# Sliding windows, 64 x 8 x 8 each, from one core: channel halves on the two partition halves, and stores of one half at a time

## Chip, cores, metric

One NeuronCore of one Trainium2 chip. The metric is the device time of one launch in microseconds; unless said otherwise, the median of several runs. Lower is better.

## The reference

```python
# x: (16, 64, 64, 64) float32;  window_size 8, stride 4  ->  n_h = n_w = 15
for i in range(15):
    for j in range(15):
        result[:, i, j] = x[:, :, 4*i : 4*i + 8, 4*j : 4*j + 8]
# result: (16, 15, 15, 64, 8, 8) float32
```

No arithmetic: 16.8 MB are read once, 59.0 MB written, since windows overlap.

## The kernel before

A partition holds one image b, one half of the channels (ch) and one quarter of the height (q): partition = 8b + 4ch + q. Loads and stores take every fourth partition, so 32 at a time, both halves together.

```python
L = lpool.tile([P, CL, RB, W], f32)          # 128 x (32 channels, 16 rows, 64)
x_v = x.rearrange("b (ch cl) (hq r) w -> hq (b ch) cl (r w)", ch=CH, hq=HQ)
for k in range(NCH):                          # 4 groups of 8 channels
    for q in range(HQ):
        nc.scalar.dma_start(out=L[q::HQ, k*cw:(k+1)*cw, :, :],
                            in_=x_v[q, :, k*cw:(k+1)*cw, :])
for j in range(NW):
    for s in range(NSLOT):                    # window row i = 4q + s
        g = gpool.tile([P, CL, WS, WS], f32, name="g")     # 9 buffers
        # ... VectorE: copy the window; for s = 3 half of it comes from
        #     the next partition by stream_shuffle ...
        for q in range(HQ):
            i = NSLOT * q + s
            if i < NH:
                nc.sync.dma_start(out=o_v[i, j, ...], in_=g[q::HQ, cs, :, :])  # 32 x 8 KB
```

## Time and profile before

| | before |
|---|---|
| time | 222.6 us (221.84 to 222.94) |
| last load packet ends | 45.8 us |
| 8 KB stores | 50.6 to 220.7 us |
| load packet, 4 KB, mean | 164 ns |
| store packet, 8 KB: median, mean | 309, 365 ns |
| store transfers | 237 |

The last five rows come from the trace's packet records (start, duration, size; no engine number). A packet's duration is the time that one of the 16 DMA engines (the page's count) spent on it; in this trace 15.3 packets are under way at a time, on average, from 60 to 200 us. The lines of the page are in the prediction.

### The profile page before, as it was taken

How to read it: one execution, taken by the hardware profiler on the slowest of the kernel's cores; microseconds unless marked ns; L12 is line 12 of the kernel's file. 1: busy time of each engine (PE TensorE's matmuls, PEld its weight loads, DVE VectorE, ACT ScalarE, POOL GpSimd, SP SyncE). 2: the span in 40 equal slices, each digit the busy share in tenths (PEclk: the TensorE clock that was granted, in tenths of full speed). 3: DMA queues.
4: the chain of work that ended last, by engine and by line, in shares of the span. 5: the costliest groups of instructions: out<-in, count | busy, mean ns of one | idle time of the engine just before them, and what ended most of it. 6: DMA issues, size and time to landing. Idle time of an engine off the chain costs nothing.

```text
span 222.1 us, 564 instructions
## 1 busy us (share of the span) xinstructions
DVE 82.9 (37%) x93; POOL 0.2 (0%) x4
## 2 busy tenths in 40 slices
DVE  0000000069946354454526453535454545430000
POOL 0000000000000000000000000000000000000000
DMA  5999999928999999999999999999999999999995
GB/s 210 418 409 412 412 413 409 412 103 285 337 356 351 328 350 344 334 344 337 341 339 348 359 341 342 353 347 335 360 353 342 332 354 334 329 347 335 326 359 215
DMA packets 15733, 75.81 MB, mean 341 GB/s; under 512 B 4049, under 2 KB 4049, under 8 KB 8657
## 3 DMA queue, kind: packets, MB, share of 16 engines
q1 hardware_dynamic: 11376, 59.00, 74.9%
q10 hardware_dynamic: 4352, 16.78, 18.9%
q14 instruction: 5, 0.03, 0.0%
HBM read 16.78 MB, written 58.98 MB: 341 GB/s over the span
## 4 chain that ended last, share of the span: by engine, by line
SPq 59%; DMA 22%; issue 5%; DVE 2%; ACTq 1%; DVEq 0%
SPq L72 59%; DMA L<-in_x_dram 20%; DMA out_dram<-g 3%; ACTq L48 1%; DVE g L64 1%; DVE g L68 1%; DVE g L67 0%; DVEq L64 0%; DVEq L67 0%
## 5 line engine op out<-in xcount | busy, mean ns | idle before, releaser
L64 DVE COPY g<-L 128x2048 f32<-128x2048 f32 (+1 forms) x48 | 55.1, 1159 | 93.2 <-DMA out_dram<-g 47.9
L68 DVE STREAM_SHUFFLE g<-L 128x1024 f32<-128x1024 f32 x15 | 19.2, 1278 | 0.0
L67 DVE COPY g<-L 128x1024 f32<-128x1024 f32 x15 | 10.4, 693 | 21.9 <-DMA out_dram<-g 21.9
L68 DVE LOAD_MASK_SELECT g<-L x15 | 0.2, 15 | 0.0
L92 POOL MEMSET const-bfloat16-1.0<- 128x1 bf16 x1 | 0.1, 102 | 0.0
L92 POOL MEMSET const-uint8-127<- 128x1 uint8 x1 | 0.1, 102 | 0.0
L92 POOL MEMSET const-float32-0.0<- 128x1 f32 x1 | 0.1, 99 | 0.2 <-issue 0.2
L92 POOL MEMSET const-float32-1.0<- 128x1 f32 x1 | 0.1, 99 | 0.0
## 6 DMA issues: line engine op xcount, KB each, us to landing
out_dram<-g SPq DMA_DIRECT2D x221, 256.0 KB, 3.8
L<-in_x_dram ACTq DMA_DIRECT2D x16, 1024.0 KB, 10.8
out_dram<-g SPq DMA_DIRECT2D x16, 64.0 KB, 5.1
```

Of the source, the lines that this page charges most:

```text
L48: nc.scalar.dma_start(out=L[q::HQ, k * cw : (k + 1) * cw, :, :], in_=x_v[q, :, k * cw : (k + 1) * cw, :],)
L64: nc.vector.tensor_copy(out=g[:, cs, :, :], in_=L[:, cs, s * ST : s * ST + WS, cols])
L67: nc.vector.tensor_copy(out=g[:, cs, 0:ST, :], in_=L[:, cs, s * ST : RB, cols])
L68: nc.vector.stream_shuffle(out=g[:, cs, ST:WS, :], in_=L[:, cs, 0:ST, cols], mask=nxt)
L72: nc.sync.dma_start(out=o_v[i, j, :, :, k * CFREE // chunks : (k + 1) * CFREE // chunks], in_=g[q::HQ, cs, :, :],)
L92: nc = _bacc.Bacc("TRN2", target_bir_lowering=False, num_devices=1)
```

## The change

Intent: give the channel half to the upper partition bit and store one half at a time, so that a transfer stays on one partition half (0 to 63 or 64 to 127); let eight of the DMA engines run one group of ten packets behind the other eight, so that the two sets of engines always use different halves; and have fewer, larger stores. That engines on different halves don't hinder each other was the assumption; the trace before has no transfer of one partition half.

```diff
-    x_v = x.rearrange("b (ch cl) (hq r) w -> hq (b ch) cl (r w)", ch=CH, hq=HQ)
+    x_v = x.rearrange("b (ch cl) (hq r) w -> ch hq b cl (r w)", ch=CH, hq=HQ)
+    def load(ch, q, k, b0=0, nb=B):
+        p0 = ch * HP + b0 * HQ + q                  # HP = 64
+        nc.scalar.dma_start(out=L[p0 : p0 + (nb-1)*HQ + 1 : HQ, cs, :, :],
+                            in_=x_v[ch, q, b0 : b0 + nb, cs, :])
+    load(0, *pieces[0], 0, HB)                      # 8 images: eight engines
+    load(0, *pieces[0], HB, HB)
+    for n in range(0, len(pieces), 2):              # then 2 of half 1, 2 of half 0, ...
+        for u in pieces[n : n + 2]:     load(1, *u)
+        for u in pieces[n + 1 : n + 3]: load(0, *u)
...
+    # store: one half of a window, 64 partitions; store_x: crossing windows, 16 partitions
+    J = NW - 1
+    g0, gx = window(J, 0), crossing([J])
+    for b0 in (0, HB):                              # 8 images: eight engines alone
+        store(g0, 0, J, 0, b0, HB)
+        store_x(gx, 0, [J], 0, b0, HB)
+    for j in range(0, J, 2):
+        js = [j, j + 1]
+        gx = crossing(js)
+        for s in range(NSLOT - 1):
+            gs = [window(u, s) for u in js]
+            for ch in (1, 0):                       # 4 + 4 + 2 = 10 packets an engine
+                for u, g in zip(js, gs): store(g, ch, u, s)
+                store_x(gx, ch, js, s)
...  # the last column likewise; window buffers 9 -> 5, two crossing buffers added
```

More of the change, by code (lines that the diff above doesn't have):

```diff
@@ L34 @@
     NSLOT = RB // ST
-    assert WS == 2 * ST
+    CFREE = CL * WS * WS
+    HB = B // 2
+    HP = P // CH
+    assert HQ == 4 and CH == 2 and WS == 2 * ST and HP == B * HQ
     lpool = ctx.enter_context(tc.tile_pool(name="lpool", bufs=1))
-    gpool = ctx.enter_context(tc.tile_pool(name="gpool", bufs=9))
+    gpool = ctx.enter_context(tc.tile_pool(name="gpool", bufs=5))
+    xpool = ctx.enter_context(tc.tile_pool(name="xpool", bufs=2))
     L = lpool.tile([P, CL, RB, W], f32)
-    x_v = x.rearrange("b (ch cl) (hq r) w -> hq (b ch) cl (r w)", ch=CH, hq=HQ)
@@ L43 @@
-    o_v = out.rearrange("b i j (ch cl) r w -> i j b ch (cl r w)", ch=CH)
+    x_v = x.rearrange("b (ch cl) (hq r) w -> ch hq b cl (r w)", ch=CH, hq=HQ)
     NCH = 4
     cw = CL // NCH
-    for k in range(NCH):
-        for q in range(HQ):
-            nc.scalar.dma_start(
-                out=L[q::HQ, k * cw : (k + 1) * cw, :, :],
-                in_=x_v[q, :, k * cw : (k + 1) * cw, :],
-            )
+    def load(ch, q, k, b0=0, nb=B):
+        cs = slice(k * cw, (k + 1) * cw)
+        p0 = ch * HP + b0 * HQ + q
+        nc.scalar.dma_start(
+            out=L[p0 : p0 + (nb - 1) * HQ + 1 : HQ, cs, :, :],
+            in_=x_v[ch, q, b0 : b0 + nb, cs, :],
+        )
@@ L53, with window @@
+    pieces = [(q, k) for k in range(NCH) for q in range(HQ)]
+    load(0, *pieces[0], 0, HB)
+    load(0, *pieces[0], HB, HB)
+    for n in range(0, len(pieces), 2):
+        for u in pieces[n : n + 2]:
+            load(1, *u)
+        for u in pieces[n + 1 : n + 3]:
+            load(0, *u)
+    o_v = out.rearrange("b i j (ch cl) r w -> ch i j b (cl r w)", ch=CH)
     nxt = [min(p + 1, 31) for p in range(32)]
-    CFREE = CL * WS * WS
-    for j in range(NW):
+    def window(j, s):
+        g = gpool.tile([P, CL, WS, WS], f32, name="g")
@@ L56 @@
         cols = slice(j * ST, j * ST + WS)
-        for s in range(NSLOT):
-            g = gpool.tile([P, CL, WS, WS], f32, name="g")
-            chunks = NCH if j == 0 and s == 0 else 1
-            n = CL // chunks
-            for k in range(chunks):
-                cs = slice(k * n, (k + 1) * n)
-                if s < NSLOT - 1:
-                    nc.vector.tensor_copy(out=g[:, cs, :, :], in_=L[:, cs, s * ST : s * ST + WS, cols])
-                else:
-                    nc.vector.tensor_copy(out=g[:, cs, 0:ST, :], in_=L[:, cs, s * ST : RB, cols])
-                    nc.vector.stream_shuffle(out=g[:, cs, ST:WS, :], in_=L[:, cs, 0:ST, cols], mask=nxt)
-                for q in range(HQ):
-                    i = NSLOT * q + s
-                    if i < NH:
-                        nc.sync.dma_start(
-                            out=o_v[i, j, :, :, k * CFREE // chunks : (k + 1) * CFREE // chunks],
-                            in_=g[q::HQ, cs, :, :],
-                        )
+        nc.vector.tensor_copy(out=g[:, :, :, :], in_=L[:, :, s * ST : s * ST + WS, cols])
@@ new lines, in window, with crossing, store @@
+        return g
+    def crossing(js):
+        g = xpool.tile([P, 2, CL, WS, WS], f32, name="gx")
+        for n, j in enumerate(js):
+            cols = slice(j * ST, j * ST + WS)
+            nc.vector.tensor_copy(out=g[:, n, :, 0:ST, :], in_=L[:, :, (NSLOT - 1) * ST : RB, cols])
+            nc.vector.stream_shuffle(out=g[:, n, :, ST:WS, :], in_=L[:, :, 0:ST, cols], mask=nxt)
+        return g
+    def store(g, ch, j, s, b0=0, nb=B):
+        p0 = ch * HP + b0 * HQ
+        o = o_v[ch, s::NSLOT, j].rearrange("q b f -> b q f")[b0 : b0 + nb]
+        nc.sync.dma_start(out=o, in_=g[p0 : p0 + nb * HQ].rearrange("p c r w -> p (c r w)"))
@@ new lines, in store_x @@
+    def store_x(g, ch, js, q, b0=0, nb=B):
+        p0 = ch * HP + b0 * HQ + q
+        o = o_v[ch, q * NSLOT + NSLOT - 1, js[0] : js[-1] + 1].rearrange("j b f -> b j f")[b0 : b0 + nb]
+        i = g[p0 : p0 + (nb - 1) * HQ + 1 : HQ, 0 : len(js)].rearrange("p j c r w -> p j (c r w)")
+        nc.sync.dma_start(out=o, in_=i)
+    J = NW - 1
[9 more added lines that the diff above has]
+            for ch in (1, 0):
+                for u, g in zip(js, gs):
+                    store(g, ch, u, s)
+                store_x(gx, ch, js, s)
@@ L79 @@
+    gx = crossing([J])
+    gs = [window(J, s) for s in range(NSLOT - 1)]
+    for ch, ss in ((1, (0, 1)), (0, (1, 2)), (1, (2,))):
+        for s in ss:
+            store(gs[s], ch, J, s)
+            store_x(gx, ch, [J], s)
 _INS = ['x', 'window_size', 'stride']
```

## The prediction

> **What bounds the kernel now.** The kernel only moves data: 16.8 MB in, 59.0 MB out, one VectorE copy between. I read first the page's parts on busy time and on the 40 slices.
>
> ```profile
> DVE 82.9 (37%) x93; POOL 0.2 (0%) x4
> ...
> DMA  5999999928999999999999999999999999999995
> GB/s 210 418 409 412 412 413 409 412 103 285 337 356 351 328 350 344 334 344 337 341 339 348 359 341 342 353 347 335 360 353 342 332 354 334 329 347 335 326 359 215
> ```
>
> VectorE is idle for 63% of the span, so it doesn't bound. The 16 DMA engines are busy in every slice but one, at two rates: about 412 GB/s while loading (slices 2 to 8), about 342 while storing (slice 11 on). Between them stands one bad slice of 103 GB/s: the last load has landed and no 8 KB store has started. Next I asked for the same by stretch of time (columns: VectorE, GpSimd, clock, DMA share, GB/s).
>
> ```profile
> 3.00:45.00 42.00, 1.28 (x3) 0.00 (x0) 1.00 1.03 412
> 45.00:51.00 6.00, 4.58 (x7) 0.00 (x0) 1.00 0.32 87
> 51.00:220.00 169.00, 77.08 (x84) 0.00 (x0) 1.00 0.96 342
> ```
>
> So 169 of the 222 us are the store stretch: engines 96% busy, yet a sixth slower than in the load. Then the chain that ended last and the waits of SyncE's queue, which issues the stores:
>
> ```profile
> SPq 59%; DMA 22%; issue 5%; DVE 2%; ACTq 1%; DVEq 0%
> ...
> SPq L72 <- DVE g L64: 33.4, 4, 13.7
> SPq L72 <- DMA out_dram<-g: 5.2, 2, 2.6
> ...
> out_dram<-g SPq DMA_DIRECT2D x221, 256.0 KB, 3.8
> L<-in_x_dram ACTq DMA_DIRECT2D x16, 1024.0 KB, 10.8
> ```
>
> SyncE issues without a stop: its waits (33.4 and 5.2 us) all lie before 51 us; from there it issues a 256 KB store every 0.76 us or so, of which the issue itself takes 0.536 at least and 0.644 at the median. 3.8 us from issue to landing over 0.76 is five stores in flight. Two limits are therefore close together: the issue (about 0.64 + 0.045 us between two = 0.68 a store) and the engines.
>
> The trace's packet records tell more. Of 7072 store packets of 8 KB, more than half take exactly 309 ns (26.5 GB/s an engine, 424 on sixteen); the mean is 365, the 90th percentile 514, the longest 944. Load packets of 4 KB: median 159 ns, mean 164, next to none above 172. So a store packet has a clean time of 309 ns and something lengthens about four in ten of them, up to double and more. It is not VectorE: after 200 us, with VectorE done, the mean is still 372 and then 357. Excess: 7072 / 16 = 442 packets an engine x (365 - 309) ns = **24.8 us**. That is what the change can win.
>
> [...] 237 stores left 3792 records of 4 bytes, 16 each.
> [...]
>
> [...] Against it: loads have the same geometry and hardly a slow packet.
>
> **The change part by part.**
> 1. *Partitions.* Channel half goes to the upper partition bit: 64 x half + 4 x image + quarter. [...]
> 2. *Groups.* Two windows (4 + 4 packets an engine) and one crossing store (2) make ten packets of a half, then ten of the other. [...]
> 3. *Stores.* 4 + 7 x 3 x 2 x 3 + 10 = 140 instead of 237. At 0.68 us that is 95 us of issuing, well below the engines' time: SyncE drops out as the second limit, and the queue becomes deeper. Packets: 7200 of 8 KB; engines 0 to 7 take 10 + 420 + 25 = 455, the others 445.
> 4. *Loads.* 33 of 512 KB or less. Engines 0 to 7 take 16 + 31 x 8 = 264 packets of 4 KB x 0.160 = 42.2 us, the others 39.7. From 2.2 us (first packet before) to 44.5; the landing came about 0.4 us after the last packet before: 44.9.
> 5. *Start of the stores.* The stores of the first window's channel chunks during the load are gone; nothing can be stored before all has landed. VectorE then makes the first window (1.23 us), one crossing (0.69 + 1.27 = 1.96), two more crossings (3.9), one window (1.23): the first full group can be issued at 44.9 + 8.3 = 53.2, and its packets start some 1.2 us after the issue (before: 49.4 to 50.6). So 54.4, against 50.6 before: 3.8 us later, only half recovered by work already done (before, 512 packets of 2 KB = 2.7 us an engine were stored by then; after, ten packets = 3.1 us on engines 0 to 7).
> 6. *Steady store.* 445 packets x 309 ns = 137.5; 136 semaphore writes x 15 ns (9 and the gap) = 2.0; first packet unhidden 0.3: 139.8. Buffers do not bind: a pair of columns takes 60 packets = 18.5 us on the engines and 2 x 1.96 + 6 x 1.23 = 11.3 on VectorE; with five window buffers each fill is about 5 us early.
> 7. *End.* 54.4 + 139.8 = 194.2, and 1.4 us from last packet to end of span (220.7 to 222.1 before) = 195.6; the timed median lies 0.5 above the profiled span: **196** if no packet collides.
>
> **Rivals.**
> - *The offset isn't there when it is needed.* By step 5 engines 0 to 7 finish their ten packets near 52, before the first full group: all engines begin it together. If sharing is fair, the offset stays zero and each packet takes 618 ns: 54.4 + 445 x 0.618 = 329 us. But in the kernel before, all 16 engines also start together (50.61 to 50.88), and the mean is 391 ns in the first 10 us and about 360 after[...]. If they do so here by ten packets, the loser stands for about 3 us once: 199.
> - *The slow packets come from writing HBM[...].* Then 365 ns stays: 54.4 + 445 x 0.365 + 3.7 = 220.5, the same time as before. In favour: loads of the same geometry run clean. Pieces in HBM also become 8 KB with jumps, where two neighbours of 16 KB followed one another.
> - *The issue starves the engines.* In favour: SyncE never waits in the store stretch and five stores are in flight, not more. Then slow packets are half-fed ones and the 140 larger stores cure them [...]: 196 to 199 again.
> - *A mix*: collisions of a tenth of the excess to a third remain: 445 x 6 to 19 ns = 3 to 8 us above 196.
>
> **The range.** Two of four stories give 196 to 199, the mix 199 to 204, HBM 220, lasting lockstep 329. That the order of groups was built so exactly for one offset speaks for the clean case, but step 5 says that the offset must form by itself. I take 199, with 192 to 218 for eight in ten; faster by over 2% (below 218.1) 0.79, same 0.08, slower 0.13.
>
> **What would show it.** Right: median store packet 309 and mean below 330; over 400 GB/s in store slices; fewer than 150 store issues and SyncE waiting on landings of stores (queue full) instead of issuing without pause; a hole of some 9 us with little traffic after about 45 us. Wrong: packet mean near 365 (HBM), near 618 at some 215 GB/s (lockstep), load slices well below 400 [...], or VectorE waits of long duration inside a pair of columns with the engines idle (buffers).

An assumption: engines that are at the same partitions at the same time hinder each other, and one a packet ahead is not hindered; what stands after "Against it" speaks against that. In the first rival "sharing" is that two such engines are held up alike, and "do so" that engines get out of step by themselves, both assumptions too; 618 is twice the clean 309.

The sum: 44.5 (end of the loads) + 9.9 (to 54.4, the first full group) + 139.8 (stores) + 1.4 (end) = 195.6, or 196, and 199 with the 3 us of the first rival. How its terms were got: packets an engine are worked out by count, so a store of 64 packets on 16 engines gives four each, and (7200 - 80) / 16 = 445. The sentence cut from step 2 gave the first four stores, of eight images each, to eight engines alone, ten packets each: the offset of one group. The trace before could not show that; the changed kernel's does: 8 records of 4 bytes for each of them in place of 16, and their 80 packets under way eight at a time. The records name no engine: "engines 0 to 7", here and in the expectations, is the name for these eight, taken to be the same each time. "Semaphore writes" are the records of 4 bytes, 9 ns each on average in the trace before; the 6 ns of gap are an estimate: from the end of one 8 KB packet to the start of the next the commonest time there is 2 to 3 ns, and a record of 4 bytes has a gap on either side.

## The result

The changed kernel takes **321.98 us** (320.97 to 327.72, 4 runs, of which the longest counts as slow and is left out of the ratio), the kernel before 222.22 us in the same rounds: 1.449 times as long, with a 95% interval of 1.437 to 1.461. (A ratio is the mean time of one kernel's fast runs over that of the other's of the same rounds, so not quite the ratio of the medians quoted.) The output is correct.

The page of the changed kernel, parts on busy time, slices, the chain that ended last, and issues (issues: count, KB each, us from issue to landing):

```profile
DVE 84.6 (26%) x94; POOL 0.2 (0%) x4
...
DMA  5999999971699999999999999999999999999997
GB/s 156 247 247 245 249 252 250 252 189 78 154 252 239 259 233 262 235 260 233 261 230 266 235 262 237 254 240 260 245 250 252 245 253 242 261 237 258 237 252 182
...
DMA 57%; SPq 17%; DVE 11%; issue 5%; ACTq 2%; DVEq 0%
...
out_dram<-g SPq DMA_DIRECT2D x89, 512.0 KB, 6.5
L<-in_x_dram ACTq DMA_DIRECT2D x31, 512.0 KB, 17.0
```

The engines are as busy as before and move only about 250 GB/s, in the loads too (412 before). The chain has turned from SyncE's issues (59% before) to the transfers (57%). By stretch of time (VectorE, GpSimd, clock, DMA share, GB/s):

```profile
2.00:45.00 43.00, 0.00 (x0) 0.00 (x0) 1.00 0.99 242
45.00:55.00 10.00, 0.00 (x0) 0.00 (x0) 1.00 1.02 244
55.00:320.00 265.00, 84.58 (x94) 0.00 (x0) 1.00 0.94 238
```

At 45 to 55 us, where the kernel before had begun to store, it is still loading at the same low rate. The packet records say what a busy engine was busy with:

| | before | after |
|---|---|---|
| load packet, 4 KB, mean | 164 ns | 264 ns |
| store packet, 8 KB, mean | 365 ns | 516 ns |
| store packets within 312 ns | 60% | 21% |
| store packets of 590 to 630 ns | 2% | 45% |
| last load packet ends | 45.8 us | 73.5 us |
| all 16 engines store from | 50.6 us | 83.1 us |
| last packet | 220.7 us | 319.3 us |

The clean packet is still 309 ns, but the commonest duration is now 596 ns, nearly its double. The 98.6 us between the two last packets divide into 27.7 in the loads (73.5 - 45.8), 4.8 in the gap before the stores (9.6 instead of 4.8) and 66.1 in the stores (236.2 instead of 170.1).

The timeline around the start of the stores (start us, duration us, what):

```profile
74.09 1.23 DVE L75 COPY g<-L 128x2048 f32<-128x2048 f32 x1 [74.09 <-DMA L<-in_x_dram]
...
75.35 0.84 SPq L90 DMA_DIRECT2D out_dram<-g  x1
...
77.15 0.68 SPq L96 DMA_DIRECT2D out_dram<-gx  x1
...
77.88 0.65 SPq L90 DMA_DIRECT2D out_dram<-g  x1
78.58 0.65 SPq L96 DMA_DIRECT2D out_dram<-gx  x1
...
80.56 5.75 DVE L75 COPY g<-L 128x2048 f32<-128x2048 f32 x5
81.80 1.73 SPq L90 DMA_DIRECT2D out_dram<-g  x2
```

The four stores for eight engines alone are issued by 79.2 us, and the packet records show eight packets under way at once, every one within 314 ns, until 80.8 us. The first store for all engines is issued at 81.80 us; its packets begin at 83.07 us on eight engines, 83.3 to 83.6 on the other eight, and from there most of them take about 596 ns (the median from 83.7 to 90 us). So eight engines on one partition half had clean packets, 8 x 8192 bytes / 309 ns = 212 GB/s, and 16 on one half packets of nearly double the time, 16 x 8192 / 596 = 220 GB/s: by this estimate from the packet times, about the same rate for the half. The offset had been worked off before it was needed. In the loads it was not: when all 16 engines became busy at 4.5 us, 81 load packets had begun. Even if all of them were of the eight engines that had begun first, ten each, these had six of their sixteen packets left. e3 and e5 below show what that was worth.

Once the stores run, SyncE is held in the act of issuing (a store of 64 partitions took 0.59 us to issue at least, 1.62 at the median and 2.26 at most):

```profile
101.24 3.46 SPq L90 DMA_DIRECT2D out_dram<-g  x2
104.75 1.76 SPq L96 DMA_DIRECT2D out_dram<-gx  x1
106.56 3.67 SPq L90 DMA_DIRECT2D out_dram<-g  x2
110.27 1.47 SPq L96 DMA_DIRECT2D out_dram<-gx  x1
```

Comparing issue ends with landings, a further store is taken only when two or three are still under way, 6 to 10 packets an engine.

### The profile page after: what moved, and what is told of

It reads as the page before. It is cut to its first block, busy times and chain, and to the rows that moved or that the text cites. A ratio compares the mean times of both kernels' runs of the same rounds, so it can differ in the third digit from the quotient of the medians.

```text
span 320.6 us, 411 instructions
## 1 busy us (share of the span) xinstructions
DVE 84.6 (26%) x94; POOL 0.2 (0%) x4
## 4 chain that ended last, share of the span: by engine, by line
DMA 57%; SPq 17%; DVE 11%; issue 5%; ACTq 2%; DVEq 0%
DMA out_dram<-g 35%; DMA L<-in_x_dram 21%; SPq L96 11%; DVE g L75 8%; SPq L90 7%; DVE gx L84 2%; ACTq L54 2%; DMA out_dram<-gx 1%; DVE gx L83 0%; DVEq L75 0%; DVEq L83 0%
## 5 line engine op out<-in xcount | busy, mean ns | idle before, releaser
L75 DVE COPY g<-L 128x2048 f32<-128x2048 f32 x46 | 56.1, 1227 | 212.0 <-DMA out_dram<-g 126.4
L84 DVE STREAM_SHUFFLE gx<-L 128x1024 f32<-128x1024 f32 x16 | 20.4, 1278 | 0.0
L83 DVE COPY gx<-L 128x1024 f32<-128x1024 f32 x16 | 10.9, 682 | 0.0
```

Source lines behind the costliest of these rows:

```text
L75: nc.vector.tensor_copy(out=g[:, :, :, :], in_=L[:, :, s * ST : s * ST + WS, cols])
L83: nc.vector.tensor_copy(out=g[:, n, :, 0:ST, :], in_=L[:, :, (NSLOT - 1) * ST : RB, cols])
L84: nc.vector.stream_shuffle(out=g[:, n, :, ST:WS, :], in_=L[:, :, 0:ST, cols], mask=nxt)
```

## The experiments

**Words.** A clean packet is one at the commonest short time (159 ns for 4 KB, 309 ns for 8 KB). A run of packets is what an engine takes from one half before it changes to the other. The offset is the number of packets by which the eight engines that take the transfers of eight images are behind the other eight. The records name no engine: packets an engine, runs and offsets are worked out by count, as estimates.

**Theory (partitions).** How long a packet takes depends on the partitions that the other engines are at in the same moment: eight engines on one partition half had packets of 309 ns in the changed kernel, 16 on it 596. Without an offset, by count, all 16 are on one half with nearly every packet. **Rivals:** the HBM addresses of one half are slow; the transfers themselves cost (their size, or those on eight engines); the starts or buffers disturb. In the expectations, a forecast that is not called a rival's, and has lost its reason, is this theory's.

Packet means of all runs, from the trace's packet records:

| run | load ns | store ns | last load us | time us |
|---|---|---|---|---|
| before | 164 | 365 | 45.8 | 222.2 |
| after | 264 | 516 | 73.5 | 322.0 |
| e1 two queues | 218 | 388 | 58.4 | 243.2 |
| e2 half in low bit | 332 | 399 | 88.1 | 288.8 |
| e3 no offset | 307 | 519 | 79.6 | 328.7 |
| e4 swap each transfer | 281 | 413 | 78.3 | 287.5 |
| e5 true offset | 234 | 517 | 64.4 | 322.4 |
| e6 half offset | 233 | 523 | 63.9 | 319.3 |
| e7 before, half loads | 299 | 363 | 80.5 | 258.2 |
| e8 before, two issuers | 164 | 367 | 45.1 | 218.9 |
| e9 offset by second queue | 274 | 524 | 73.3 | 325.4 |
| e10 full-width stores (wrong) | 165 | 316 | 44.3 | 191.6 |
| e11 half-width stores (wrong) | 164 | 509 | 44.1 | 289.8 |
| e12 eighths of the height | 126 (2 KB) | 1026, 836 (16 KB) | 64.5 | 318.1 |
| e13 ready windows, no offset (wrong) | 165 | 509 | 44.1 | 289.9 |
| e14, e15 (void, see below) | 164 | 508, 502 | 44.2 | 289.1, 287.0 |
| e16 as e13, offset, same queue | 165 | 503 | 44.2 | 289.8 |
| e17 as e13, offset, second queue | 165 | 506 | 44.2 | 288.5 |

e1, e5, e8 and e12 were timed in three rounds; the others are single runs, whose state is therefore unknown, and nothing below 3% is read from them. Identical loads vary, too: the changed kernel, e9 and e4 have the same ones, at 264, 274 and 281 ns. The trace of e12 is from an execution (320.69 us).

**e1: two queues.**

```diff
-        nc.scalar.dma_start(out=L[...])            # loads
+        (nc.scalar, nc.sync)[ch].dma_start(out=L[...])
-        nc.sync.dma_start(out=o, ...)              # both kinds of stores
+        (nc.sync, nc.scalar)[ch].dma_start(out=o, ...)
```

> Only the queue changes: the transfers of channel half 1 are issued from ScalarE where half 0's are issued from SyncE (stores), and the other way round for the loads; layout, sizes, addresses and order within a half are those of the changed kernel. [...] loads back near 400 GB/s and done by about 46 us, store packets a mean of 310 to 380 ns, whole time 195 to 230 us. Rival 'per-transfer cost or the 8-engine transfers slow everything': same transfers, so still about 320 us. Rival 'HBM addresses of one half at a time': can't be told apart here, the mix of addresses changes as well.

Measured 243.16 us, 1.092 times before (1.086 to 1.098). Loads and stores of the page:

```profile
GB/s 169 283 313 313 314 314 318 312 301 125 119 294 290 305 361 314 339 340 348 347 349 368 324 353 330 334 351 345 337 343 347 310 348 353 340 365 317 343 322 178
```

Loads rose from about 247 to 313 GB/s, stores from about 248 to some 340. The same transfers in the same layout are faster when each half has a queue of its own (load packets 218 ns for 264, store packets 388 for 516): a cost of the transfers themselves is out. It is a partial miss: loads did not come back to 400 and the time stayed above 230.

**e2: half in the lowest bit.**

```diff
-        p0 = ch * HP + b0 * HQ + q        # load; stores likewise, step HQ -> HQ * CH
+        p0 = (b0 * HQ + q) * CH + ch
-    nxt = [min(p + 1, 31) for p in range(32)]
+    nxt = [min(p + CH, 31) for p in range(32)]
```

> Only the SBUF layout changes: the channel half is the lowest partition bit (partition = 8 x image + 2 x quarter + half) instead of bit 6. Every transfer, its HBM addresses, size, engine count, order and queue stay as in the changed kernel; a store of a half now reads every second partition of all 128[...]. [...] the 596 ns packets go; the mean store packet is below 420 ns, loads above 330 GB/s, whole time 200 to 260 us. Rival 'HBM addresses of one half at a time' and rival 'per-transfer cost': nothing of theirs changed, so 516 ns a packet and 320 us.

Measured 288.84 us: stores much better (399 ns for 516), loads worse (332 for 264). The expectation was wrong about the loads, instructively. A load takes partition 8b + 2q + half of each image b, so 16 partitions, one in eight, and the offset of the first loads did not help: 332 ns is 2.1 times 159, the clean load packet. So it is not the partition half alone that counts; why one partition in eight is slow was not shown. Not one HBM address or transfer was changed, and both rates moved, in opposite directions: the place in SBUF moved them. The rival of HBM addresses is out.

```profile
GB/s 102 174 207 208 206 203 207 206 203 207 208 187 58 171 304 331 324 295 316 330 320 301 305 315 295 322 313 301 304 323 300 307 329 317 307 312 330 324 279 211
```

Slices 3 to 11 are loads at 203 to 208 GB/s, half of the 412 before.

**e3: no offset.**

```diff
-    load(0, *pieces[0], 0, HB)
-    load(0, *pieces[0], HB, HB)
+    load(0, *pieces[0])
-    for b0 in (0, HB):
-        store(g0, 0, J, 0, b0, HB); store_x(gx, 0, [J], 0, b0, HB)
+    store(g0, 0, J, 0); store_x(gx, 0, [J], 0)
```

> The first load and the first stores of the changed kernel run on all 16 engines instead of on engines 0 to 7 in two parts; nothing else changes. [...] in the changed kernel engines 0 to 7 entered the loads some 5 to 6 packets of 16 behind (1.65 x 159 = 262 ns, measured 264). Without that the load packets go to 2 x 159 = 318 ns, loads end near 84 us instead of 73.5. The stores began together anyway (the offset had run out), so their mean stays near 516 ns: whole time 326 to 334 us. Rival 'the 8-engine transfers are what costs': faster than 300 us.

Measured 328.72 us; loads 307 ns, stores 519. As expected: the parts on eight engines bought some load time and nothing in the stores. The five to six packets of offset worked out for the loads of the changed kernel fit the six or more that the eight engines of its first loads still had to take when the others began. The page of e3, loads at 213 to 222 GB/s:

```profile
GB/s 169 217 214 219 218 222 213 221 220 143 104 237 244 251 247 245 261 235 259 238 258 237 254 242 256 250 244 257 233 261 236 260 228 268 238 255 251 243 250 188
```

**e4: swap the half after each transfer.**

```diff
-            for ch in (1, 0):
-                for u, g in zip(js, gs): store(g, ch, u, s)
-                store_x(gx, ch, js, s)
+            for u, g in zip(js, gs):
+                for ch in (1, 0): store(g, ch, u, s)
+            for ch in (1, 0): store_x(gx, ch, js, s)
```

> Only the order of stores changes: the half swaps after each transfer (runs of 4, 4, 4, 4, 2, 2 packets an engine) instead of after ten packets. Loads as in the changed kernel (73.5 us). If at each swap a fixed number of packets, three to four, runs at 309 ns [...], runs of 4 leave next to no slow ones: mean 310 to 370 ns, whole time 235 to 260 us. If the share of slow packets belongs to the halves or the addresses and not to the length of a run: still 516 ns and 320 us.

Measured 287.54 us; stores 413 ns. Shorter runs of packets cost less, so the length of a run matters, with addresses and layout unchanged. The figures were missed (310 to 370 ns, 235 to 260 us): runs of 4, 4 and 2 packets are not nearly clean.

**e5 and e6: make the offset.** The first pair of columns is prepared first, then six window stores and two crossing stores (e5) or four and two (e6) go to eight engines ahead; the first two loads, also for eight engines, carry 13 channels instead of 8.

```diff
-    g0, gx = window(J, 0), crossing([J])
-    for b0 in (0, HB): ...
+    gx0, gxJ = crossing([0, 1]), crossing([J])
+    early = [window(J, s) for s in range(3)]
+    g00 = [window(u, 0) for u in (0, 1)]
+    for s, b0 in [(0,0), (0,8), (1,0), (1,8), (2,0), (2,8)]:   # e6: the first four
+        store(early[s], 0, J, s, b0, HB)
+    for b0 in (0, HB): store_x(gxJ, 0, [J], 0, b0, HB)
```

> The offset of one group is really made. Loads: the first two loads (engines 0 to 7 alone) carry 13 channels each, 26 packets an engine, of which some 11 are done when engines 8 to 15 start, so 15 of a run of 16 remain. Stores: the first pair of columns is prepared before anything is stored, then six window stores and two crossing stores go to engines 0 to 7 (26 packets, 8 issues of about 0.64 us = 17 packets of time), so 9 to 10 of a group of ten remain when the first full group starts. Groups of ten and everything else as in the changed kernel. [...] loads 160 to 185 ns a packet, done near 46 us; store packets 309 to 350 ns on average; whole time 198 to 218 us. Rival 'a half at a time is slow by itself (addresses, transfers)': still about 500 ns and 310 us or more. If the queue cannot hold so many stores for engines 0 to 7, the offset comes out smaller and the mean lies between.

> As the run with the true offset, but only four window stores and two crossing stores go ahead to engines 0 to 7: 18 packets less 6 issues of time leave 5 to 6 packets of ten. Loads as there. [...] a share of (10 - 5.5) / 10 of the packets is slow, 309 x 1.45 = 448 ns on average, in 400 to 470; whole time 250 to 285 us. Rival, in which the offset settles at the same value from wherever it starts: the same mean as in the run with the true offset, or the 516 ns of the changed kernel.

Measured 322.37 us (1.449 times before, 1.442 to 1.456) and 319.3 us; stores 517 and 523 ns, the mean of the changed kernel, wherever they started. Timeline of e5:

```profile
71.84 5.67 SPq L94 DMA_DIRECT2D out_dram<-g  x6
77.56 2.47 SPq L100 DMA_DIRECT2D out_dram<-gx  x2
...
80.12 5.52 SPq L94 DMA_DIRECT2D out_dram<-g  x4
```

The six stores for eight engines took 5.67 us to issue, lengthening from about 0.7 to 1.15 us each, and the full stores could only be issued at 80.12 us. By the packet records, packets are clean (309 ns) until 81 us and 596 to 604 ns from then: the ahead packets had been eaten while SyncE was held. So for the stores these runs don't show whether an offset is kept, since hardly any existed.

The loads did get a larger offset, and the gain lasted. By count, the eight engines had done the first of their two loads, 13 packets of 26, by 4.5 to 5.1 us, about when the others began. From then on a load packet took 234 ns on average (e6, with the same loads: 233), to the end of the loads:

| load packets, mean ns | 8 to 24 us | 24 to 40 us | 40 to 56 us |
|---|---|---|---|
| e3: no offset | 312 | 305 | 309 |
| changed kernel: six or seven packets | 271 | 271 | 267 |
| e5: about thirteen packets | 241 | 234 | 234 |

```profile
GB/s 174 280 278 276 287 289 291 234 37 168 226 235 244 247 247 236 244 248 242 254 227 258 231 259 232 261 231 254 234 257 232 256 235 251 234 257 235 251 241 169
```

So in the loads of these runs what a lead given once was worth did not fade from 8 to 56 us (241, 234, 234 ns in e5), though even in e5 only some 45% of the packets took 175 ns or less. Loads also queue deeper: comparing issue ends with landings, ScalarE took a further load of e3 with seven under way, 56 packets an engine.

**e7: half loads in the kernel before.**

```diff
+            for ch in range(CH):
                 nc.scalar.dma_start(
-                    out=L[q::HQ, k*cw:(k+1)*cw, :, :],
-                    in_=x_v[q, :, k*cw:(k+1)*cw, :],
+                    out=L[ch*HQ + q :: HQ*CH, k*cw:(k+1)*cw, :, :],
+                    in_=x_v[q, ch::CH, k*cw:(k+1)*cw, :],
```

> The kernel before, with each of its 16 loads cut in two by channel half: 16 partitions a load[...], instead of 32[...]. Layout, stores and bytes stay. [...] load packets go from 164 to about 320 ns, the loads end near 85 us instead of 46, stores as before (365 ns), whole time 255 to 268 us. Rival, in which loads were slow in the changed kernel for the offset or for the new layout alone: 164 to 180 ns, 222 to 228 us.

Measured 258.17 us; loads 299 ns, done at 80.5 us; stores 363 ns as before. One part of the change alone, taking the halves apart in a load, reproduces the slow loads without the new layout and without any offset. Such a load has 16 partitions, one in eight, as in e2 (332 ns); a load of the kernel before has 32, one in four (164 ns).

**e8: two issuers in the kernel before.** The store goes to `(nc.sync, nc.scalar)[q % 2]` instead of `nc.sync`.

> The kernel before, with every second store issued from ScalarE instead of SyncE; nothing else. If the issue of stores (0.68 us of 0.76 a store) starves the engines, this takes it away: store packets near 309 to 330 ns and 198 to 208 us. If the 365 ns come from engines [...], packets stay between 350 and 390 ns and the time within 3% of 222 us.

(The last forecast is for engines that hinder each other.)

Measured 218.9 us, 0.983 of before (0.978 to 0.987); store packets 367 ns. Issuing does not starve the engines; the 1.7% are an earlier start (48.5 us instead of 50.6) and a store stretch of 167.4 us instead of 170.1, with the same packets in it. It is the fastest correct version here; at a threshold of 2% the verdict on it is unclear.

**e9: the ahead packets on a second queue.** The first pair is prepared first; the four ahead stores of the changed kernel are issued from ScalarE.

> The changed kernel with its ten ahead packets (the four stores to engines 0 to 7 alone) issued from ScalarE, and made after the first pair of columns[...]. Loads as in the changed kernel. Theory 'the offset is lost because SyncE's queue holds only two or three stores (6 to 10 packets), so no engine can be a group of ten behind another for long': the ten packets do delay engines 0 to 7, but the queue pulls the offset back; store packets stay between 430 and 525 ns, 285 to 325 us. Rival 'only the start was wrong, an offset once made stays': 309 to 350 ns and 230 to 250 us.

Measured 325.44 us; stores 524 ns. It doesn't decide: VectorE stood 8.45 us for a window buffer before 93.3 us, the stores ran dry, and when all engines were busy again, at 94 us, packets took about 597 ns as before.

**e10 and e11: the cost alone.** Wrong on purpose: loads, layout and VectorE work of the kernel before, but windows go to the output one after the other, 1 MB each: in e10 by one store of 128 partitions, in e11 by its two halves, those of two windows in turn.

```diff
-                for q in range(HQ): ... nc.sync.dma_start(out=o_v[i, j, ...], in_=g[q::HQ, cs, :, :])
+    put(made(n), 4*n, 4)                                   # e10: 128 partitions, 1 MB in a row
+    for h in (1, 0):                                       # e11: 64 partitions
+        for k, g in enumerate(gs): put(g, 4*(n+k) + 2*h, 2, 64*h)
```

> A wrong result on purpose, to measure one cost alone: loads, layout and VectorE work of the kernel before, but each window leaves in one store of all 128 partitions to 1 MB in a row of the output (the right bytes in number, at the wrong places), 56 stores and a quarter. [...] mean store packet 309 to 325 ns, over 400 GB/s while storing, 190 to 204 us. If HBM writing or the SBUF side as a whole sets the 365 ns of the kernel before: 350 to 380 ns and 212 to 225 us.

> As the run with full-width stores, wrong on purpose too and to the same places of the output, but each store cut in its two partition halves and the halves of two windows taken in turn: upper, upper, lower, lower, so runs of eight packets an engine. [...] with about three packets of each run free: 309 x (2 - 3.3 / 8) = 490 ns, in 450 to 560; 262 to 300 us. If the halves are slow in the changed kernel for the HBM addresses that they write[...]: as the full-width run, within 5%.

Measured 191.59 us with 316 ns a packet (36 of 7200 above 360), and 289.83 us with 509 ns. Page of e10, then of e11:

```profile
DMA  5999999993999999999999999999999999999996
GB/s 180 404 414 410 413 407 410 413 407 129 414 420 414 414 426 416 418 420 420 420 420 418 418 421 418 426 418 414 420 420 423 418 421 418 420 418 425 418 420 231
```

```profile
DMA  6999995999999999999999999999999999999996
GB/s 258 411 412 410 410 410 126 236 237 257 257 239 250 255 247 240 255 254 241 251 251 245 245 256 249 236 259 254 242 243 256 249 233 259 251 237 254 251 242 156
```

The same bytes to the same places: 418 GB/s in full-width stores, some 248 in half-width ones taken in turn, at equally busy engines. This is the change's own loss in the stores, without its layout, loads, buffers or crossing stores. One more thing differs: SyncE took the full-width stores in 0.33 us with seven of them under way, the half-width ones in about 2 us with two. That did not leave engines idle in e11 (busy share 9 in all store slices but the last).

**e12: a correct layout with full-width stores.** For this trial the partition became 8 x image + eighth of the height, with all 64 channels in it.

In short form, not the code itself:

```diff
+    L[:, c] <- x[:, c] as (b hq) x (r w)                  # 64 loads, 128 partitions
+    out[:, 0::2, j] <- g          # 128 partitions x 16 KB, SyncE
+    out[:, 2a+1::8, j] <- g[a::4]  # a = 0..2, 32 partitions, ScalarE;  out[:, 7, j] <- g[3::8]
```

> A correct kernel in another layout, as a trial of what the clean full-width run suggests: partition = 8 x image + eighth of the height, all 64 channels in a partition, so half of the windows (even rows) leave in stores of all 128 partitions, 16 KB each, and six of the seven odd rows in stores of 32 partitions (every fourth, as in the kernel before), the seventh in one of 16 partitions (every eighth). Loads: 64 of one channel, all 128 partitions, 2 KB packets, from both queues. [...] loads near 45 to 50 us, even rows clean at twice 309 ns for 16 KB, odd rows as before, whole time 198 to 215 us. [...] mean well over 700 ns for 16 KB, 225 to 280 us.

(The first forecast is for full-width stores as clean as those of e10, the second for engines that hinder each other on them.)

Measured 318.14 us, 1.418 times before. Packets of 16 KB took 1026 ns on SyncE's queue, where 611 was the commonest value. So 128 partitions are not enough: here the output side starts with 16 images, where e10 writes 1 MB in a row, and the clean packets of e10 do not come. Why was not shown. The time was missed by more than the packets explain.

**e13 to e17: can an offset stay?** Their outputs are wrong, which doesn't matter for the times. e11 with four windows made once and stored over and over, so that neither VectorE nor a buffer can hold a store back.

In short form:

```diff
+    gs = [made(n) for n in range(4)]                       # e13
+    for m in ahead:                                        # e14: 4 stores, nc.sync; e15: 2, nc.scalar
+        nc.sync.dma_start(out=<32 rows in a row>, in_=gs[0][0:32])
# e16, e17: as e14, e15, the rows as eight pieces of four with gaps
```

> Wrong on purpose. The half-width run with four windows made once and stored over and over: no waiting for VectorE or for buffers, runs of eight packets a half, all 16 engines begin together. If a third of a run comes clean because VectorE and the buffers disturb the step, lockstep is now complete: near 596 ns a packet, store stretch 265 us, 315 us in all. If it comes from the engines and the queue: as the half-width run, 490 to 525 ns, 280 to 295 us.

Measured 289.85 us, 509 ns: like e11, so that not all packets are slow does not come from VectorE or the buffers.

> As the run without offset, but four stores of 32 partitions go ahead on SyncE to engines 0 to 7 alone: 16 packets, half of which are worked off while they are issued, so up to eight of a run of eight should remain. If the short queue of stores eats the offset: within 4% of the run without offset. If an offset stays when nothing else disturbs it: below 400 ns, 215 to 240 us.

> As the run without offset, but two stores of 32 partitions (eight packets for engines 0 to 7 alone) go out from ScalarE beside the first full stores of SyncE. If an offset stays once it is there: 309 to 350 ns, 195 to 215 us. If the short queue pulls the engines together: within 4% of the run without offset.

Both are void for the question (289.1 and 287.0 us): the ahead stores left 16 records of 4 bytes each, as a store for all 16 engines does (16 each in the kernel before), not 8. Their rows followed one another in the output, in one stretch; in e16 and e17, where the same rows lie as eight pieces with gaps, 8 records each were left.

> Wrong on purpose. As the run with finished windows and no offset (509 ns a packet, 289.9 us), but four stores go ahead on SyncE to engines 0 to 7 alone (eight records of 4 bytes each in the trace, or the run is void): 16 packets, half of them worked off while they are issued. If the short queue of stores eats the offset: 490 to 525 ns. If an offset stays: below 400 ns, 215 to 240 us.

> Wrong on purpose. As the run with finished windows and no offset, but two stores (eight packets, engines 0 to 7 alone, eight records of 4 bytes each or the run is void) go out from ScalarE beside the first full stores of SyncE. If an offset stays once it is there: 309 to 350 ns, 195 to 215 us. If engines are pulled together again: 490 to 525 ns after at most two groups, 283 to 292 us.

Here eight records each were left. Measured 289.77 us with 503 ns, and 288.53 us with 506 ns. In e16 eight engines work alone from 47.5 us, every packet clean, and have by my estimate (4 us at 309 ns each) about three of their sixteen packets left when the others join between 51 and 52. In e17 the ahead packets are worked off among the full ones from 49.9 to 54.7 us, while packets average 420 to 500 ns by the microsecond, so by count (the records name no engine) the eight engines are then eight behind. In both, microseconds with means of 600 to 700 ns and of 360 to 450 ns alternate soon after, as in e13. So in these stores an offset of three packets (e16) and, by count, one of eight (e17) changed nothing after a few groups. What pulls the stores to the same mean stays open, and so does why loads keep an offset and stores don't. That SyncE takes a further half-width store only with two or three under way, which leaves no room for a lag of ten packets, while seven loads are under way, fits and is not shown to be the cause: loads also differ in direction and packet size.

## Why the prediction was wrong

*The sum, term by term.* The loads were to end at 44.5 us and ended at 73.5: the term "264 packets of 4 KB x 0.160" was 264 ns a packet in fact, two thirds more. The offset of the loads was six or seven packets of a run of sixteen, not the whole run (e3, e5). The gap from the last load to the first full group was worked out as 9.9 us (54.4 - 44.5) and was 9.6: right, with the hole named. The stores were to take 139.8 us and took 236.2: the term "445 packets x 309 ns" was 516 in place of 309. The end, 1.4 us, was 1.3. Counts were right: 140 stores, and 2208 records of 4 bytes are 136 x 16 + 4 x 8, so the first four ran on eight engines as said.

*The step that failed.* The first rival had the start and nearly the time: all engines begin together, each packet takes 618 ns, 329 us. (The 329 was right in part by luck: it had clean loads and stores at 618, and left out the 3.7 us of semaphore writes and end that the HBM rival counts; in fact the loads lost 28 us, and store packets took 516 ns, a quarter of them 360 or less.) I set it aside with the assumption that engines get out of step by themselves (no trace shows it) and: "If they do so here by ten packets, the loser stands for about 3 us once". The first half was read into the kernel before, where the mean falls from 391 ns in the first 10 us to some 363 after; what makes it fall was not shown. The second was carried over to runs of ten packets without support. e4 shows the length of the run counting (413 ns in runs of 4, 4, 2; 516 in runs of ten), and e13, e16 and e17 that the mean stays at 503 to 509 ns wherever the engines start. As an estimate from the clean 309 and the mean of 509 (e13), 309 x (2 - 0.35) = 510: it is as if about a third of a run of eight, some three packets, came clean and the rest took double, and no more.

*The second failed step* was to hold loads harmless: "Against it: loads have the same geometry and hardly a slow packet". They had it only as long as a load covered both halves. Cut apart in e7 they go from 164 to 299 ns. Why a load of 32 partitions has clean packets and one of 16 does not, the records don't show. The prediction had listed "load slices well below 400" among its signs of being wrong, but gave it no share of the range; the slices were near 247.

*The offset.* The prediction saw that it would be used up before the first full group (step 5), then still gave 0.79 to a gain, on the hope that it would form by itself. A device that the prediction's own schedule shows to be missing should have been counted as missing: the forecast would have had two peaks, near 196 and near 329.

*The other rivals.* HBM writing is out as cause of the new loss (e2, e11 against e10). Starved engines are out as the cause of the 365 ns before (e8). Whether the 365 ns of the kernel before come from engines that meet as well is likely after e10 (316 ns) but not shown: e10 writes other addresses.

## What to carry to other kernels

Look at which partitions all DMA engines read or write in the same moment, not at how many partitions a transfer has: in the stores of the changed kernel packets took nearly twice the time (596 for 309 ns) with 16 engines on one partition half as with eight, at full "busy"; loads of 16 partitions, one in eight, took 299 ns where those of 32, one in four, took 164 (e7, before); and a store of all 128 partitions was clean in e10 (316 ns for 8 KB) and not in e12 (1026 for 16 KB). A scheme that relies on engines being out of step has to be tested on the transfers that are to use it: in the stores a lead given at the start was gone within a few groups in both runs that made one (e16, e17), in the loads it lasted and was worth 307 - 234 = 73 ns a packet (e3, e5). Safer than a lead, in these runs, were stores that take every fourth of all 128 partitions (as before: 365 ns), or all 128 to one stretch of the output (e10: 316 ns).
